# The gate columns as rows of the low-rank blocks, and the small products of the recurrences' chains in unbroken groups

## Chip, cores and metric

The kernel runs on one core of one Trainium2 chip. The metric is the device time of one launch in microseconds (us), as the median of the runs shown. The engines are TensorE (PE; its weight loads are listed apart as PEld), VectorE (DVE), ScalarE (ACT), GpSimd (POOL) and SyncE (SP), which issues most of the transfers.

## The reference, cut to what matters

Two blocks follow one another on a sequence of 512 tokens of width 2048. The first has a convolution branch and a differential attention and is not touched. The second joins a gated delta rule (GDN, 8 heads of 128) and an RWKV-7 recurrence (16 heads of 64), each in both directions, and each first over a context of 256 tokens and then, with the state that it left, over the 512 latent tokens:

```python
u = h @ w_in[layer]              # 512 tokens: GDN q, k, v, z (4 x 1024), 32 gate columns,
uc = hc @ w_in[layer]            # then RWKV r, k, v (3 x 1024), 4 x 96 low-rank columns, z
...
gates = u[..., 4 * D_GDN:].astype(jnp.float32).reshape(b, n, 2, 2, GDN_HEADS)
g = -jnp.exp(a_log) * jax.nn.softplus(gates[:, :, 0] + dt_bias)
beta = jax.nn.sigmoid(gates[:, :, 1])
...
def step(state, inp):            # gated delta rule, one chunk
    u_i, wk_i, attn_i, q_i, k_i, gl_i = inp
    v_new = u_i - wk_i @ state
    o_i = q_i @ state + attn_i @ v_new
    state = state * jnp.exp(gl_i)[..., None, None] + jnp.einsum('bhcd,bhce->bhde', k_i, v_new)
...
wd = xs[..., lo:lo + 2 * LORA_W].reshape(b, n, 2, LORA_W)     # RWKV: low-rank columns
ad = xs[..., lo + 2 * LORA_W:].reshape(b, n, 2, LORA_A)
w_log = -jax.nn.softplus(-(w0 + jnp.einsum('bndr,drc->bndc', jnp.tanh(wd), w_up))) - 0.5
a = jax.nn.sigmoid(a0 + jnp.einsum('bndr,drc->bndc', ad, a_up))
...
def step(state, inp):            # RWKV, one token; xs are mixed with their grid neighbours
    r_t, w_t, k_t, v_t, kk_t, b_t = inp
    sa = -jnp.einsum('bhvk,bhk->bhv', state, kk_t)
    state = (state * w_t[:, :, None, :] + sa[..., None] * b_t[:, :, None, :]
             + v_t[..., None] * k_t[:, :, None, :])
    return state, jnp.einsum('bhvk,bhk->bhv', state, r_t)
```

## The kernel before

**Dense products.** Every product with the weights `w_in` goes by `products` (L122 to L138) in blocks of 128 columns: SyncE loads half a block of weights (`wraw`), ScalarE rounds it (`whi`, L104) and VectorE takes the rest (`wlo`, L105; in the context stage every second one is GpSimd's, `K.on_pool = 2`). For each of the 16 tiles of 128 input rows, three products at L136 follow: whi by the high part of the activation, whi by its low part, wlo by the high part. A block is therefore 48 products of 128x512 (latent, activation `big`) or 128x256 (context, activation `hc`). `w2_cols` (L1756) makes 69 blocks of the second block's columns: one for the 32 gate columns (`B_GATE`, the other 96 columns empty), eight each for q, k, v, z of GDN and r, k, v of RWKV, four for the low-rank columns (`B_LO`, 96 columns and 32 empty ones each), eight for z of RWKV.

**The order.** A list scheduler puts each engine's instructions in order: of those whose inputs would be ready it takes the one with the lowest priority number, and that number grows along the program text. Dense products have `ahead = FIRST` for all but the first of a burst (6 or 12 products), so a burst stays together; small products of the chains have no such tie and are placed one by one between bursts. Each engine then runs its list strictly in that order.

**Gates.** `gdn_gates` (L420 to L517) takes a gate block from PSUM: VectorE adds the bias (gg_x, L425), works out softplus and logarithms by polynomials (L170 to L178, L427 to L444), makes a running sum over 64 tokens (L452 to L462) and writes three inputs gg_R (L467; L486 to L488 with ScalarE) of the transposes on TensorE (L497 to L499). Everything of the GDN chains waits on them.

**Low-rank blocks.** `rwkv_lora` (L793 to L799) mixes each block with its neighbours (ScalarE L771, VectorE L789) and puts the result aside. In the context stage the gate block comes first (L1697 to L1700), then K and V of GDN (`ctx_dense_gdn`), then the GDN chains, and behind them the low-rank blocks at the head of `ctx_dense_rwkv` (L1284). In the latent stage the gate block and the first low-rank block are multiplied while the activation is still being modulated (`K.pre`, L1450: PSUM banks px0 and pc); then follow gates, three low-rank blocks, and q, k, v, z head by head (`mixers_gdn`, L1485).

**GDN chains** (`gdn_core`, L700 to L758). A step takes 128 tokens in each direction: products with the state (L722), R on VectorE, products with the inverse (L728), vn on VectorE, products for the new state (L737), the state update on VectorE, and in the latent stream the output in a bank `po`: with the state (L751) and with vn (L752).

**RWKV chains** (`step` in `rwkv_pair`, L983 to L1058). One step takes 64 tokens of two heads (u) in both directions (d): four first products with the state H into bank `pc` (L1007), in the latent stream four output products into `po` (L1013), a copy X (ScalarE, L1016), four products with the inverse (L1032), H scaled by VectorE (L1034) and ScalarE (L1035), four products for the next state (L1039), four updates on VectorE that write the next H (L1047), and four more output products (L1052). There are 64 such steps in the latent stream and 32 in the context. Beside them the scheduler has the inversions of the next unit (L375, L381, 32x32), transposes (L931), 64x128 products (L964) and dense blocks to place. On the page each of the 64x64 products of these lines shows as two records.

## Time and profile before

| | |
|---|---|
| time, median of 3 runs | 3996.94 us (3995.03 to 4008.11) |
| profiled execution, its own time | 4009.06 us |
| span of that execution | 4007.3 us |
| busy: TensorE / VectorE / ScalarE / GpSimd | 3749.4 / 2758.9 / 1364.2 / 497.6 us |
| dense products of the first and second block together (L136), records with activation big | 5344 with whi, 2800 with wlo |
| mean granted clock of TensorE | 0.958 of full speed |

The profile lists one execution; all its times are microseconds from the span's start. A timeline row gives the start, how long from the first record's start to the last one's end, engine, line, tiles and the number of records; in brackets, where there is one, the idle time of that engine before it and what ended it. Matmul records overlap their successors, so what a product costs in the queue is the distance from its start to the next one's start. In the context stage the program runs from about 440 to 1580 us of the span, the latent front from 2200 to 2320, the latent chains from there on, RWKV's mostly from 3000 to 3890.

### The profile page before, as it was taken

Reading aid. Unit: us, or ns where it says so; the run is one execution under the profiler, and the core shown is the slowest. Engines: PE = TensorE matmul, PEld = TensorE weight load, DVE = VectorE, ACT = ScalarE, POOL = GpSimd, SP = SyncE. Lnnn points to the kernel's source line nnn. Section 1 sums busy time; section 2 is a strip of 40 time slices with the busy share of each in tenths; the row PEclk is TensorE's granted clock in tenths of the full one; section 3 lists DMA queues with packets and bytes.
Section 4 is the critical chain, followed back from the end, with each engine's and each line's share of the span. In section 5 each row is a group of like instructions: output and inputs, shape, how many; then the busy total and the mean of one; then the engine's idle time right before and its main releaser. Section 6 shows DMA issues by size and latency. Waiting matters only on the chain. (4 is left out here: it accounts for less than half of the span.)

```text
span 4007.3 us, 81999 instructions
## 1 busy us (share of the span) xinstructions
PE 3749.4 (94%) x33162; PEld 2890.2 (72%) x33162; DVE 2758.9 (69%) x7151; ACT 1364.2 (34%) x2707; POOL 497.6 (12%) x592
## 2 busy tenths in 40 slices
PE   8899779998999999999998799999999999999997
PEld 4577678876767677777886578777877777677776
DVE  3366897798777777643533977676667886777866
ACT  2322334322334434332322332232323443444433
POOL 0100230013100100000311201100001111110102
PEclk9899999999999999999999999999999998999999
DMA  8765445423324333524623232222223211122236
GB/s 318 259 231 212 155 135 168 146 100 112 120 79 142 108 110 110 168 85 163 210 95 125 98 103 71 68 71 68 83 80 108 68 65 56 67 72 89 98 124 203
DMA packets 206780, 495.05 MB, mean 124 GB/s; under 512 B 40129, under 2 KB 71361, under 8 KB 202305
## 3 DMA queue, kind: packets, MB, share of 16 engines
q1 hardware_dynamic: 206400, 489.81, 36.0%
q8 instruction: 260, 4.26, 0.4%
q14 instruction: 120, 0.97, 0.1%
HBM read 436.64 MB, written 53.09 MB: 122 GB/s over the span
## 5 line engine op out<-in xcount | busy, mean ns | idle before, releaser
L136 PE MATMUL pd<-big,whi 128*128 128x512 f32 x5344 | 1784.5, 412 | 9.3 <-ACT big L331 8.0
L136 PEld LDWEIGHTS pd<-big,whi 128*128 128x128 f32 x5344 | 980.5, 193 | 256.6 <-issue 20.4
L136 PE MATMUL pd<-big,wlo 128*128 128x512 f32 x2800 | 1120.1, 400 | 6.6 <-DVE wlo L105 6.2
L104 ACT CAST whi<-wraw 128x1024 fp32r<-128x1024 f32 (+2 forms) x500 | 506.7, 1014 | 1156.9 <-PE pd L136 1079.8
L105 DVE TENSOR_TENSOR wlo<-wraw,whi 128x1024 fp32r<-128x1024 f32 (+2 forms) x483 | 580.8, 1202 | 321.7 <-ACT whi L104 309.7
L136 PEld LDWEIGHTS pd<-big,wlo 128*128 128x128 f32 x2800 | 538.2, 192 | 130.6 <-DVE wlo L105 10.0
L136 PE MATMUL pd<-hc,whi 128*128 128x256 f32 x1184 | 229.5, 293 | 19.5 <-ACT gc_up L541 6.5
L136 PEld LDWEIGHTS pd<-hc,whi 128*128 128x128 f32 x1184 | 189.1, 195 | 24.1 <-ACT gc_up L541 7.2
L136 PE MATMUL pd<-hc,wlo 128*128 128x256 f32 x592 | 172.7, 292 | 25.8 <-DVE wlo L105 21.5
L136 PE MATMUL pd<-ext,whi 128*128 128x512 f32 x512 | 184.2, 400 | 3.9 <-DVE ext L105 3.8
L1133 DVE SCALAR_TENSOR_TENSOR cv_y<-cv_up,vec,cv_y 128x512 f32<-128x512 f32 x240 | 180.6, 752 | 4.4
L136 PE MATMUL pd<-fa,whi 128*128 128x512 f32 x448 | 149.9, 415 | 0.4 <-DVE wo L1520 0.2
L136 PEld LDWEIGHTS pd<-hc,wlo 128*128 128x128 f32 x592 | 115.3, 195 | 31.5 <-DVE wlo L105 25.1
L1029 ACT ACTIVATE rg_zw<-rg_H,rg_wc 64x64 f32<-64x64 f32 x320 | 104.6, 343 | 48.8 <-DVE rg_H L1047 43.4
L136 PEld LDWEIGHTS pd<-ext,whi 128*128 128x128 f32 x512 | 97.0, 190 | 27.8 <-DVE ext L105 4.8
L1047 DVE SCALAR_TENSOR_TENSOR rg_H<-pc,rg_wc,rg_zw 64x64 f32<-64x64 f32 x320 | 90.4, 283 | 35.7 <-PE pc L1039 27.1
L221 DVE SCALAR_TENSOR_TENSOR ada_ev<-wraw,cs_ada,ada_ev 128x512 f32<-128x512 f32 x120 | 90.7, 756 | 31.1 <-DMA wraw<-in_wada_dram 29.6
L546 DVE SCALAR_TENSOR_TENSOR gc_y<-gc_up,vec,gc_y 128x512 f32<-128x512 f32 (+1 forms) x160 | 106.8, 668 | 2.5
L916 POOL TENSOR_TENSOR rg_bk<-rg_th,rg_L 64x512 f32<-64x512 f32 x48 | 67.9, 1414 | 311.3 <-ACT rg_L L895 170.8
L136 PEld LDWEIGHTS pd<-fa,whi 128*128 128x128 f32 x448 | 80.3, 190 | 20.1 <-issue 1.4
L964 PE MATMUL px<-rg_C,rg_bk 64*128 64x128 f32 x512 | 90.5, 305 | 0.2 <-DVE rg_C L967 0.2
L1424 POOL TENSOR_TENSOR sgl<-sgl 128x512 f32<-128x512 f32 x16 | 33.9, 2118 | 448.1 <-ACT whi L104 441.2
(583 smaller groups left out, 5679.1 us busy)
## 6 DMA issues: line engine op xcount, KB each, us to landing
wraw<-in_w_dram SPq DMA_DIRECT2D x372, 512.0 KB, 3.6
wraw<-in_wada_dram SPq DMA_DIRECT2D x128, 512.0 KB, 4.6
wraw<-in_wada_dram SPq DMA_DIRECT2D x32, 1024.0 KB, 4.9
wraw<-in_wo_dram SPq DMA_DIRECT2D x32, 512.0 KB, 3.4
sgl<-sgd SPq DMA_DIRECT2D x48, 256.0 KB, 3.4
wraw<-in_wout_dram SPq DMA_DIRECT2D x20, 512.0 KB, 4.0
wraw<-in_w_dram SPq DMA_DIRECT2D x32, 256.0 KB, 3.6
sgd<-msg SPq DMA_DIRECT2D x32, 256.0 KB, 3.3
```

The source lines that it names most:

```text
L104: K.nc.scalar.copy(hi, src)
L105: (eng or K.nc.vector).tensor_tensor(lo, src, hi.bitcast(F32), op=ALU.subtract)
L136: nc.tensor.matmul(ps[:, :T], lhsT=a[:, k], rhs=b, start=(n == 0), stop=(n == 3 * (k1 - k0) - 1))
L221: nc.vector.scalar_tensor_tensor(ev, raw[:, k], cs[:, kk, 0:1], ev, op0=ALU.mult, op1=ALU.add)
L546: nc.vector.scalar_tensor_tensor(y, up[:, t:t + T], w[:, t:t + 1], y, op0=ALU.mult, op1=ALU.add)
L916: nc.gpsimd.tensor_tensor(bk[uq, :, u], th[uq], F[uq], op=mul)
L964: nc.tensor.matmul(pg[:, m], lhsT=bk[q, 4 * r + m].rearrange("p x c -> p (x c)"), rhs=C[q, 4 * r + m, u], start=True, stop=True, tile_posi ...
L1029: nc.scalar.activation(zw[hv[u], d], H[hv[u], ms[d], u], AF.Copy, scale=wn[hv[u], 4 * d + mn])
L1047: nc.vector.scalar_tensor_tensor(Hn[hv[u], 4 * d + mn, u], pc3[hv[u], 2, d], wn[hv[u], 4 * d + mn], zw[hv[u], d], op0=mul, op1=ALU.add)
L1133: nc.vector.scalar_tensor_tensor(y, up[:, t:t + 512], w[:, t:t + 1], y, op0=ALU.mult, op1=ALU.add)
L1424: nc.gpsimd.tensor_tensor(g, g, q, op=ALU.add)
```

## The change

**The gate columns move.** The block `B_GATE` is gone. Its 32 columns stand in the empty columns 96 to 103 of the four low-rank blocks, eight in each: decay gates of the two directions in the first two blocks, beta gates in the other two. `rwkv_lora` copies PSUM rows 96 to 127 of each block into a tile `gates` with ScalarE and mixes rows 0 to 95 as before. So the low-rank blocks come before the gates: in the context stage at the very front (`ctx_lora`), ahead of K and V; in the latent stage three of them (`PRE = 3`: banks px0, px1, pc) are multiplied during the modulation, and the fourth first thing afterwards. The second block has 68 weight blocks instead of 69.

**Small products are tied.** A class `Visit` issues the products of a group so that all but the first have `FIRST` (the scheduler takes them at once) and hang on the first by a dependence that orders without a semaphore. In RWKV the groups are L1007 with L1013, L1032 alone, L1039 with L1052; in GDN L722, L728, and L737 with L751 and L752. Within a group the order of d and u (j) is reversed, so that the product whose operand is written last comes first. `Visit.mm` is L123 of the changed kernel, and lines move: L136 is L157 there, L105 is L106, L381 is L402, L425 is L446, L497 to L499 are L518 to L520, L789 is L814.

```diff
+PRE = 3
-B_GATE, B_Q, B_K, B_V, B_Z, B_RR, B_RK, B_RV, B_LO, B_RZ = 0, 1, 9, 17, 25, 33, 41, 49, 57, 61
+B_Q, B_K, B_V, B_Z, B_RR, B_RK, B_RV, B_LO, B_RZ = 0, 8, 16, 24, 32, 40, 48, 56, 60
...
+class Visit:
+    def __init__(self, K):
+        self.K, self.first = K, None
+
+    def mm(self, *a, **kw):
+        tc = self.K.tc
+        ahead = FIRST if self.first else 0
+        tc.cur_priority -= ahead
+        i = self.K.nc.tensor.matmul(*a, **kw).ins
+        tc.cur_priority += ahead
+        if self.first:
+            tc.add_manual_dep(i, self.first.name, mybir.DependencyInfo(mybir.DependencyClass.NoSync,
+                                                                       mybir.DependencyReason.DATA), reason="visit")
+        else:
+            self.first = i
...
+        vis = Visit(K)
         if not (lat and fin):
             p = bank()
-            for d, j in chains:
-                nc.tensor.matmul(reg(p, d, j), lhsT=ktl[:, d, j, ts[d]], rhs=vn[d, j], start=True, stop=True)
+            for d, j in reversed(chains):
+                vis.mm(reg(p, d, j), lhsT=ktl[:, d, j, ts[d]], rhs=vn[d, j], start=True, stop=True)
+        if lat:
+            po = K.po.tile([128, 512], F32, name="po")
+            for d in (1, 0):
+                vis.mm(reg(po, d, 0), lhsT=vn[d, 0], rhs=at[:, d, ts[d]], start=True, stop=False)
+                vis.mm(reg(po, d, 0), lhsT=S[0][d], rhs=egt[:, d, 0, ts[d]], start=False, stop=True)
...
-def rwkv_lora(K, pool, blocks, T, s, put):
+def rwkv_lora(K, pool, blocks, T, s, put, gates):
     for j in range(4):
-        w = rwkv_mix(K, pool, blocks(B_LO + j), T, s, 3072 + 96 * j, 96, K.v["mulo"][:, j:j + 1], "rm", bufs=2)
+        ps = blocks(B_LO + j)
+        K.nc.scalar.copy(gates[32 * j:32 * j + 32], ps[96:128])
+        w = rwkv_mix(K, pool, ps, T, s, 3072 + 96 * j, 96, K.v["mulo"][:, j:j + 1], "rm", bufs=2)
...
-        for d in range(2):
-            for u in range(2):
-                nc.tensor.matmul(pc3[hv[u], 0, d], lhsT=C[:, ms[d], u, 0:64], rhs=H[:, ms[d], u], start=True, stop=True)
+        order = [(d, u) for d in (1, 0) for u in (1, 0)]
+        vis = Visit(K)
+        for d, u in order:
+            vis.mm(pc3[hv[u], 0, d], lhsT=C[:, ms[d], u, 0:64], rhs=H[:, ms[d], u], start=True, stop=True)
         if lat:
...
+            for d, u in order:
+                vis.mm(po[d][hv[u]], lhsT=H[:, ms[d], u], rhs=C[:, ms[d], u, 64:128], start=True, stop=False)
...
+        vis = Visit(K)
         if not fin:
...
+            for d, u in order:
+                vis.mm(pc3[hv[u], 2, d], lhsT=bt[:, ms[d], hv[u]], rhs=H[:, ms[d], u], start=True, stop=True)
+        if lat:
+            for d, u in order:
+                vis.mm(po[d][hv[u]], lhsT=H[hv[u], ms[d], u], rhs=ra[hv[u], ms[d]], start=False, stop=True,
+                       tile_position=(64 * u, 64 * u))
...
-            K.pre = {b: p.tile([128, 512], F32, name=n) for b, p, n in ((B_GATE, K.px, "px0"), (B_LO, K.pc, "pc"))}
+            K.pre = {B_LO + j: p.tile([128, 512], F32, name=n) for j, (p, n) in
+                     enumerate(((K.px, "px0"), (K.px, "px1"), (K.pc, "pc"), (K.pc, "pc"))[:PRE])}
...
-            gates = gdn_gates(K, pool, kp, blk(B_GATE), 512, "lat")
+            g = pool.tile([128, 512], F32, name="gates")
+            run(rwkv_lora(K, pool, blk, 512, "lat", lambda j, w: K.dma.dma_start(K.ld[:, j], w[:96]), g))
+            gates = gdn_gates(K, pool, kp, g, 512, "lat")
...
-                    K.gc = gdn_gates(K, pool, cl, blk(B_GATE), 256, "ctx")
+                    ctx_lora(K, blk, cl, pool)
                     ctx_dense_gdn(K, blk, pool)
...
-    g=-np.ones(128,int); 
-    for kind in range(2):
-        for d in range(2): g[64*kind+32*d:64*kind+32*d+8]=4096+16*kind+8*d+np.arange(8)
-    L.append(g)
...
-        x=-np.ones(128,int); x[:96]=R+3072+96*j+np.arange(96); L.append(x)
+        x=-np.ones(128,int); x[:96]=R+3072+96*j+np.arange(96); x[96:104]=4096+8*j+np.arange(8); L.append(x)
```

TensorE's list at one step of a latent RWKV chain (the bank pc_32152 is the step's, po_32157 and po_32160 are its output banks, rg_H its state, rg_C its factors, px1 a bank of an inversion), before:

```order
L381 MATMUL px1_32367<-iv_u32_32335,iv_y_32368 32x32 x19
L1007 MATMUL pc_32152<-rg_H_31419,rg_C_31406 64x64
L1013 MATMUL po_32157<-rg_C_31406,rg_H_31419 64x64
L1007 MATMUL pc_32152<-rg_H_31419,rg_C_31406 64x64
L1013 MATMUL po_32157<-rg_C_31406,rg_H_31419 64x64
L381 MATMUL px1_32367<-iv_u32_32335,iv_y_32368 32x32 x6
L1007 MATMUL pc_32152<-rg_H_31419,rg_C_31406 64x64
L1013 MATMUL po_32160<-rg_C_31406,rg_H_31419 64x64
L381 MATMUL px1_32367<-iv_u32_32335,iv_y_32368 32x32
L1007 MATMUL pc_32152<-rg_H_31419,rg_C_31406 64x64
L1013 MATMUL po_32160<-rg_C_31406,rg_H_31419 64x64
L381 MATMUL px1_32367<-iv_u32_32335,iv_y_32368 32x32 x6
```

The same step in TensorE's list now (its bank is pc_32052, its output banks po_32057 and po_32058; L123 is the tied product, L157 the dense one, L402 the inversion):

```order
L157 MATMUL pd_33054<-big_20583,wlo_33057 128x512
L123 MATMUL pc_32052<-rg_H_31319,rg_C_31306 64x64 x4
L123 MATMUL po_32058<-rg_C_31306,rg_H_31319 64x64 x2
L123 MATMUL po_32057<-rg_C_31306,rg_H_31319 64x64 x2
L402 MATMUL px1_32267<-iv_u32_32235,iv_y_32268 32x32 x17
L123 MATMUL pc_32052<-rg_X_32063,iv_u64_31561 64x64 x4
```

Eight products that stood in three places among the pieces of the inversion stand in one place now, behind a dense burst, and the inversion is no longer cut by them.

VectorE's list at the start of the latent gate arithmetic (big is the modulated activation, wlo a split of weights, gg_x the first step of the gates), before:

```order
L332 SCALAR_TENSOR_TENSOR big<-or_n,mod_ada_85,big 128x512
L105 TENSOR_TENSOR wlo<-wraw,whi 128x512
L105 TENSOR_TENSOR big<-or_n,big 128x512
L105 TENSOR_TENSOR wlo<-wraw,whi 128x512
L425 TENSOR_SCALAR gg_x<-px_20533,vec 64x512
L427 SCALAR_TENSOR_TENSOR gg_ax<-gg_x 64x512
```

Now (rm is a mixed low-rank block, gates the collected gate rows):

```order
L106 TENSOR_TENSOR big<-or_n,big 128x512
L794 TENSOR_SCALAR rm_omu<-vec 96x1 x2
L106 TENSOR_TENSOR wlo<-wraw,whi 128x512 x5
L814 SCALAR_TENSOR_TENSOR rm<-px_20477,vec,rm 96x448
L794 TENSOR_SCALAR rm_omu<-vec 96x1
L446 TENSOR_SCALAR gg_x<-gates,vec 64x512
L448 SCALAR_TENSOR_TENSOR gg_ax<-gg_x 64x512
L814 SCALAR_TENSOR_TENSOR rm<-px_20478,vec,rm 96x448
```

The gates' first step stands behind more splits of weights and behind the mix of the first low-rank block, and takes its input from a tile in place of a PSUM bank.

TensorE's list at the latent gate transposes (px are their banks, pd a dense block's), before, where the first two are followed by dense products again:

```order
L136 MATMUL pd<-big,wlo 128x512
L497 MATMUL px_20911<-cst,gg_R_20882 128x128
L497 MATMUL px_20916<-cst,gg_R_20882 128x128
L136 MATMUL pd<-big,whi 128x512 x2
L136 MATMUL pd<-big,wlo 128x512
```

And now, the first seven of them:

```order
L157 MATMUL pd<-big,wlo 128x512
L518 MATMUL px_21020<-cst,gg_R_20991 128x128
L518 MATMUL px_21025<-cst,gg_R_20991 128x128
L519 MATMUL px_21020<-cst,gg_R_20992 128x128
L519 MATMUL px_21025<-cst,gg_R_20992 128x128
L520 MATMUL px_21020<-cst,gg_R_20993 128x64
L520 MATMUL px_21025<-cst,gg_R_20993 128x64
L518 MATMUL px_21030<-cst,gg_R_20991 128x128
```

All twelve transposes stand together now, behind six blocks and more of the dense products, where ten of the twelve stood behind further dense products before.

## Rows read from the trace of the kernel before

**Rows 1.** Page, part 1: busy us of each engine, share of the span, instructions.
```profile
PE 3749.4 (94%) x33162; PEld 2890.2 (72%) x33162; DVE 2758.9 (69%) x7151; ACT 1364.2 (34%) x2707; POOL 497.6 (12%) x592
```
**Rows 2.** By stage: length, busy PE PEld DVE ACT POOL, granted clock, DMA share, GB/s.
```profile
440.00:640.00 200.00, 152.04 (x1103) 142.11 (x1104) 171.46 (x376) 74.99 (x124) 56.82 (x67) 0.91 0.42 138
...
2200.00:2320.00 120.00, 96.34 (x352) 66.95 (x351) 105.64 (x174) 46.78 (x67) 29.05 (x28) 0.90 0.34 109
...
3000.00:3700.00 700.00, 668.53 (x8784) 501.31 (x8782) 538.79 (x1607) 295.45 (x710) 91.36 (x80) 0.94 0.22 74
```
**Rows 3.** Timeline of TensorE, a latent RWKV step cut in three.
```profile
3302.64 0.34 PE L1007 MATMUL pc<-rg_H,rg_C 128*64 128x64 f32 x4
...
3303.03 0.31 PE L381 MATMUL px<-iv_u,iv_y 32*32 32x32 f32 x12
...
3303.82 0.33 PE L1007 MATMUL pc<-rg_H,rg_C 128*64 128x64 f32 x2
...
3304.20 0.31 PE L381 MATMUL px<-iv_u,iv_y 32*32 32x32 f32 x12
```
**Rows 4.** Timeline of TensorE, a latent RWKV step in one piece between dense products.
```profile
3329.06 0.40 PE L136 MATMUL pd<-big,wlo 128*128 128x512 f32 x1
3329.39 0.45 PE L1007 MATMUL pc<-rg_H,rg_C 128*64 128x64 f32 x8
...
3330.01 0.73 PE L136 MATMUL pd<-big,whi 128*128 128x512 f32 x2
```
**Rows 5.** Timeline of TensorE, a latent gated-delta step's third group.
```profile
2405.56 0.39 PE L136 MATMUL pd<-big,wlo 128*128 128x512 f32 x1
2405.79 0.61 PE L737 MATMUL pc<-gd_vn,gd_ktl 128*128 128x128 f32 x4
2406.23 0.39 PE L752 MATMUL po<-gd_at,gd_vn 128*128 128x128 f32 x2
2406.45 0.39 PE L751 MATMUL po<-gd_egt,S 128*128 128x128 f32 x2
```
**Rows 6.** By line and shape: busy us, mean ns of one, idle before, releaser.
```profile
L1047 DVE SCALAR_TENSOR_TENSOR rg_H<-pc,rg_wc,rg_zw 64x64 f32<-64x64 f32 x320 | 90.4, 283 | 35.7 <-PE pc L1039 27.1
```
**Rows 7.** Timeline of TensorE, two triples of a context low-rank block.
```profile
628.66 0.40 PE L136 MATMUL pd<-hc,whi 128*128 128x256 f32 x2
...
629.01 0.40 PE L136 MATMUL pd<-hc,whi 128*128 128x256 f32 x2
```
**Rows 8.** Timeline of ScalarE, context: last V block's copy, last low-rank block's mix.
```profile
604.38 0.37 ACT L541 COPY gc_up<-pd 128x256 f32<-128x256 f32 x1
...
634.31 0.47 ACT L771 ACTIVATE rm<-pd,rm_omu 96x256 f32<-96x256 f32 x1
```
**Rows 9.** Dense products with hc alone: length, busy TensorE, granted clock, DMA.
```profile
466.00:601.00 135.00, 97.07 (x717) 0.92 0.39 129
```
**Rows 10.** Timeline of TensorE, the context's first gate transposes.
```profile
501.07 0.69 PE L497 MATMUL px<-cst,gg_R 128*128 128x128 f32 x2 [5.95 <-DVE gg_R L467]
```
**Rows 11.** Timeline of VectorE, first step of the context's gate arithmetic.
```profile
461.50 0.48 DVE L425 TENSOR_SCALAR gg_x<-pd,vec 64x256 f32<-64x256 f32 x1 [0.60 <-PE pd L136]
```
**Rows 12.** Timeline of TensorE, latent front from the modulation's end to the transposes.
```profile
2262.52 0.61 PE L136 MATMUL pd<-big,whi 128*128 128x512 f32 x2
...
2264.66 0.62 PE L136 MATMUL pd<-big,whi 128*128 128x512 f32 x2
...
2296.66 0.62 PE L136 MATMUL pd<-big,whi 128*128 128x512 f32 x2
...
2302.15 0.69 PE L497 MATMUL px<-cst,gg_R 128*128 128x128 f32 x2 [4.66 <-DVE gg_R L467]
2302.49 1.20 PE L136 MATMUL pd<-big,whi 128*128 128x512 f32 x2
```
**Rows 13.** Timelines of VectorE and ScalarE, first and last step of the latent gates.
```profile
2260.06 0.74 DVE L425 TENSOR_SCALAR gg_x<-px,vec 64x512 f32<-64x512 f32 x1 [1.39 <-issue]
...
2305.51 0.63 ACT L488 ACTIVATE gg_R<-gg_tl 64x512 f32<-64x512 f32 x1 [0.58 <-DVE gg_tl L485]
```

More of the change, by code (lines that the diff above doesn't have):

```diff
@@ L726, in gdn_core @@
         p = bank()
-        for d, j in chains:
-            nc.tensor.matmul(reg(p, d, j), lhsT=uu[:, d, j, ts[d]], rhs=R[d, j], start=True, stop=True)
+        vis = Visit(K)
+        for d, j in reversed(chains):
+            vis.mm(reg(p, d, j), lhsT=uu[:, d, j, ts[d]], rhs=R[d, j], start=True, stop=True)
         vn = {}
@@ L733, in gdn_core @@
         new = {}
+        vis = Visit(K)
         if not (lat and fin):
             p = bank()
[L736 to L737 removed]
+            for d, j in reversed(chains):
+                vis.mm(reg(p, d, j), lhsT=ktl[:, d, j, ts[d]], rhs=vn[d, j], start=True, stop=True)
[4 more added lines that the diff above has]
+                vis.mm(reg(po, d, 0), lhsT=S[0][d], rhs=egt[:, d, 0, ts[d]], start=False, stop=True)
+        if not (lat and fin):
             for d, j in chains:
@@ L1050, in step @@
             for d in range(2):
-                for u in range(2):
-                    nc.tensor.matmul(po[d][hv[u], 0:64], lhsT=H[hv[u], ms[d], u], rhs=ra[hv[u], ms[d]], start=False,
-                                     stop=True, tile_position=(64 * u, 64 * u))
                 ot = osum[:, 64 * k:64 * k + 64] if d == 0 else osum[:, T - 64 * k - 64:T - 64 * k][:, ::-1]
                 if k < nch // 2:
-                    nc.scalar.copy(ot, po[d][:, 0:64])
+                    nc.scalar.copy(ot, po[d])
                 else:
-                    nc.vector.tensor_tensor(ot, po[d][:, 0:64], ot, op=ALU.add)
+                    nc.vector.tensor_tensor(ot, po[d], ot, op=ALU.add)
     def out():
```

54 lines of the change are left out of this document (22 added, 32 removed).

## Prediction

> **What bounds the kernel now.** The page comes first: TensorE is busy 94% of the span, the next engine, VectorE, 69% [rows 1]. A busy share is an average, so the second view is the table by stage [rows 2]; its columns to watch are TensorE, VectorE and the granted clock. In the long stage that holds the latent RWKV chains beside dense products (3000 to 3700 us) TensorE is busy 668.5 of 700 us, 96%, and VectorE 77%: what leaves TensorE's queue there shortens the kernel. Two short stages differ. From 440 to 640 us (the context's dense products) TensorE is busy 76% and VectorE 86%; from 2200 to 2320 us (norm, modulation, gate arithmetic of the latent stream) it is 80% and 88%. There a product taken from TensorE may only uncover VectorE. So the change is costed in three terms: the ties in the chains, the context's gate block, the latent gate block.
>
> **Term 1, the ties.** They add no instruction and take none away; they change the order of TensorE's queue. What a cut costs is read from a step that is cut in three [rows 3]: first products and first output products (L1007, L1013) stand as three visits between pieces of an inversion (L381). The first visit lasts 3303.03 - 3302.64 = 0.39 and the last 3304.20 - 3303.82 = 0.38 us; with the second, of as many records as the last, taken at 0.38 it is 1.15 together. The same sixteen records in one piece last 3330.01 - 3329.39 = 0.62 us [rows 4]. So two visits fewer save 0.53 us, 0.26 each. The way in costs as well: from the last dense product before the visit to its first record it is 3329.39 - 3329.06 = 0.33 us, where dense follows dense after a third of a triple, 0.68 / 3 = 0.23 us [rows 12]. With 0.10 to 0.14 for that a removed visit is worth up to 0.40 us. The number of visits I counted in both orders, a visit being an unbroken run of the products of one group: in the latent RWKV chains the first group stands in 124 visits before and 76 now, the second in 72 and 65, the third in 74 and 64; in the context's, the first in 63 and 33, the second in 35 and 32, the third in 32 both times. That is 98 fewer. At 0.26 it is 25.5 us, at 0.40 39 us. I take 26, the low end, since a removed visit whose neighbours then are dense and inversion pays the way in there all the same.
>
> The gated-delta chains are tied too (third group 64 visits to 32 in the latent stream). What a cut costs there has a row of its own: four products L737, then L752, L751, L752 and the next step's L722 and L751 go in between two dense pieces [rows 5], each pair of records taking 0.22 us (2406.45 - 2406.23), and the first starts 2405.79 - 2405.56 = 0.23 us after a dense product, as a dense product would. A cut of these products costs nothing that the rows show, so I put 0 us for this part; its upper bound is the 0.14 us above times 43 visits, 6 us.
>
> The Trainium skill, in TensorEngine Tiling (Array Packing), section Key Properties, says that a change of the array's tiling mode, not merely of the tile, drains the engine. By that rule the price hangs on changes of shape (128*128, 128*64, 64*64, 32*32), the gated-delta half (128*128, as the dense products) is worth nothing, and the third group keeps a change inside it however it is tied. Counted by shape, the orders hold 1741 changes before and 1566 now; 175 at about 0.15 us would be 26 us. The trace agrees in [rows 3] against [rows 5].
>
> Does a tie make TensorE wait? It runs its queue in order, so a group stands still until its last operand is there. The four updates that feed the next step take 283 ns each on VectorE [rows 6], and the tied group starts with the product whose operand is written last. Where it stands in the queue is counted from the orders: between a latent step's third group and the next step's first, 3.4 dense and 4.2 other products on average stand ahead of the first cut before, 4.2 and 6.5 ahead of the last cut; now 5.2 and 10.4 stand ahead of the whole group. So the group has gone to where its last cut stood or behind it; I put 0 for new waits and keep a rival for it. No engine's work is queued behind a new semaphore: the tie orders without a wait.
>
> **Term 2, the context's gate block.** The block of 48 products is gone, and the four low-rank blocks move ahead of the K and V blocks. A triple of dense products takes 0.355 us there (629.01 - 628.66), a block 16 times that, 5.7 us [rows 7]. Behind the V blocks the four low-rank blocks now stand from about 604.4 us (the last V block's copy gc_up) to 634.3 (the last mix) [rows 8]: 29.9 us, of which 4 x 5.7 = 22.8 is product time. That stretch goes. At the front TensorE has room: of the 135 us from 466 to 601 it spends 97.1 in dense products [rows 9], and its longest single wait there, 5.95 us at the gate transposes, is for VectorE [rows 10]. What the four blocks cost at the front is therefore VectorE's time. The gate arithmetic runs from 461.50 [rows 11] until the transposes at 501.07. By the placement of the gate columns its first step needs only the first two low-rank blocks (they carry the decay gates), so it starts later by less than one block, some 5 us; in its stretch VectorE's order now has five splits instead of four and three mixes more, 1.2 + 3 x 0.6 = 3 us. So the front ends 8 us later, and everything behind it too. Net: 8 - 22.8 = -14.8, at most 8 - 29.9 = -22; I take -15, because what follows has its own uneven start.
>
> **Term 3, the latent gate block.** A triple takes (2296.66 - 2264.66) / 47 = 0.68 us, a block 10.9 [rows 12]. Before, two blocks are multiplied during the modulation, then three low-rank blocks and six products of Q; then TensorE waits 4.66 us for gg_R [rows 12]. Now three low-rank blocks go during the modulation, then the fourth, the Q and the K block, and then the gate transposes, all twelve together. The third block adds 10.9 us to the modulation, of which some 3 us fill TensorE's gaps there: its end moves from 2262.52 to about 2270.4, and TensorE stands at the transposes at 2270.4 + 32.7 = 2303.1. VectorE's arithmetic from gg_x to gg_R took 2302.1 - 2260.06 = 42.0 us [rows 12, 13], with seven splits and three mixes among it; the new order has seven and three again. It starts some 7 us later, so gg_R is there at about 2309, and the last of the three inputs 4 us after it (2305.51 + 0.63 against 2302.15): TensorE waits until 2313, 10 us instead of 4.66. By then it has done 288 products that stay in the program, before it had 198 at 2302.15. 90 x 0.227 = 20.4 us of work for 10.9 us more time: a gain of 9.5 us; I take 9. Bounds: 2 us (arithmetic behind the fourth mix) and 14 (the wait as short as before). A long wait costs clock: after the 4.66 us the next pair of products lasts 1.20 us where a pair lasted 0.62 before [rows 12], which is the lower of the two levels; about 2 us of this is in the bounds.
>
> **What costs nothing.** Eight small copies of the gate rows on ScalarE, busy 34% [rows 1]; two blocks of weights (1 MB each) less to load, on a DMA share of 0.22 to 0.42 in these stages [rows 2].
>
> **Sum.** 26 + 15 + 9 = 50 us. The profiled execution took 4009.06 us, so its like would take 3959; the median before is 3996.94, and from it the forecast is 3997 - 50 = **3947 us**. Own range of this case: ends of the terms, 3930 to 3967.
>
> **Rivals.**
> - *The ties pay nothing.* If what costs is leaving the dense stream at all, then the ties don't do what they say: the stretches of small products between dense ones are 746 before and 756 now. Likewise if the time saved comes back as waits for the chains. Against it: the pieces in [rows 3] stand between small products and still cost. Left is 15 + 9 = 24: 3973 us.
> - *More than counted.* The way in is saved too (39 us), the whole 29.9 us goes in the context stage (22), and the latent block is fully gained (11): 72 us, 3925 us.
> - *The blocks are taken back and the ties half paid:* VectorE's arithmetic decides both front stages, the two terms give 24 - 24 = 0 and the ties 10: 3987 us.
> - *Slower: tied groups wait for their last operand.* Place: the first group of each of the 96 RWKV steps. If the group stands where its first piece stood, TensorE idles for three further updates, 3 x 0.283 = 0.85 us, 82 us over all; with 50 gained that is 3997 + 32 = 4029 us. It decides from 0.5 us of wait a step on. For it: VectorE, whose L1047 writes the state that L1007 reads, itself stands idle for TensorE's L1039 for 27.1 us in all [rows 6], so this loop is closed without slack in places. Against it: the counts above. The Trainium skill, TensorE: Matmul & The Clock Gate, Part 3, states that matmuls start and end strictly in program order; no row here shows otherwise.
>
> **How the numbers follow.** Forecast 0.55, ties pay nothing 0.19, more 0.12, taken back 0.07, slower 0.07. About 0.3% (12 us) is what a measurement of this kernel can tell from no change, that is 3985 to 4009. Faster beyond that are the first three, less a little for their edges: 0.85; the fourth makes most of 0.08 for no change; slower 0.07. A range of 8 in 10 must reach from the third case to the second and past its edge: 3920 to 3985; it leaves out the last two and the lower edge.
>
> **What would show it.** Right: first groups of eight and eight records in one piece lasting 0.62 us nearly everywhere; the last V copy of the context some 8 us later and the first mix of the RWKV blocks right behind it; a wait of about 10 us at the latent gate transposes; idle time before the tied products not above some 20 us in sum. Wrong: idle time before the tied products of 0.5 us a step or more, a lower granted clock from 3000 to 3700 us than 0.94, or a VectorE so late in the two fronts that the transposes wait 20 us and more.

## The result and the profile after

The changed kernel takes 3956.01 us (median of 6 runs, 3948.75 to 3974.94) where the kernel before took 4005.62 on the same occasion (6 runs, 3995.03 to 4012.71): a ratio of 0.989, 95% interval 0.9866 to 0.9914, or 44 us less by the ratio; the two medians lie 49.6 us apart. The forecast was 50 us less, 3947 us, in a range of 3920 to 3985. A second measurement of both kernels gave 0.9894 (0.9875 to 0.9914).

The page's first part and the table by stage of the changed kernel, to be laid beside [rows 1] and [rows 2] (length, busy PE, PEld, DVE, ACT, POOL, granted clock, DMA share, GB/s):

```profile
PE 3672.7 (93%) x33066; PEld 2837.3 (72%) x33066; DVE 2748.4 (70%) x7146; ACT 1359.4 (34%) x2713; POOL 505.4 (13%) x595
```
```profile
440.00:640.00 200.00, 160.38 (x1133) 150.09 (x1133) 167.25 (x327) 78.46 (x130) 64.35 (x68) 0.91 0.42 138
2200.00:2320.00 120.00, 107.15 (x454) 84.39 (x455) 95.59 (x188) 47.23 (x69) 14.90 (x25) 0.91 0.34 104
3000.00:3700.00 700.00, 650.16 (x9191) 487.19 (x9190) 567.18 (x1662) 298.41 (x734) 104.03 (x86) 0.95 0.23 75
```

TensorE is fuller in the two short stages (160 for 152 us, 107 for 96), as the moved blocks should make it, and emptier in the stage of the latent RWKV chains (650 for 668.5 us). There a fixed window holds other work in each kernel. The whole stage, from the last product of the gated-delta chains to the last of the RWKV chains, holds the same work; before and after:

```profile
3010.00:3888.00 878.00, 839.82 (x10975) 625.98 (x10973) 676.11 (x1965) 365.59 (x883) 112.55 (x96) 0.95 0.24 80
```
```profile
2965.00:3825.00 860.00, 804.00 (x10964) 603.35 (x10964) 673.17 (x1964) 360.39 (x880) 116.40 (x96) 0.95 0.24 80
```

TensorE is busy 36 us less, and the stage is 18 us shorter. What left the queue came back only in part as shorter time: the rest is waiting.

**Two measures that the rest needs.** The six runs of the changed kernel differ by 26 us, and the mean granted clock that each run lists goes with it. The profiled execution, and that of a second measurement of the same kernel (span and clock):

```profile
core 0: 3947.0 us, clock 0.962
```
```profile
core 0: 3969.0 us, clock 0.957
```

Time multiplied by clock was 3796 to 3803 us in all six runs, while the time went from 3949 to 3975. So for each kernel I give the *weighted time*, time by clock, as the mean of its runs less that of the runs of before beside them (standard errors 1 to 3 us). It compares the lists of instructions as if at one clock; a list that lowers its own clock gains nothing by that, so what is faster is decided by the plain ratio, which holds both. From each trace I also take *TensorE's work*, its busy stretches each multiplied by the clock granted there (the first 12 to 15 us of the span have no clock record; the 3 to 6 busy us in them are left out), and its *idle time*, the span less the busy time. Before: 3612.6 and 257.8 us. After: 3557.2 and 274.2, so 55.4 us less work and 16.4 us more waiting.

### The profile page after: what moved, and what is told of

It reads as the page before. It is cut to its first block, busy times and chain, and to the rows that moved or that the text cites. A ratio compares the mean times of both kernels' runs of the same rounds, so it can differ in the third digit from the quotient of the medians.

```text
span 3947.0 us, 81802 instructions
## 1 busy us (share of the span) xinstructions
PE 3672.7 (93%) x33066; PEld 2837.3 (72%) x33066; DVE 2748.4 (70%) x7146; ACT 1359.4 (34%) x2713; POOL 505.4 (13%) x595
## 5 line engine op out<-in xcount | busy, mean ns | idle before, releaser
L157 PE MATMUL pd<-big,whi 128*128 128x512 f32 x5280 | 1759.5, 411 | 8.0 <-ACT big L352 8.0
L157 PEld LDWEIGHTS pd<-big,whi 128*128 128x128 f32 x5280 | 964.4, 192 | 251.4 <-issue 20.8
L157 PE MATMUL pd<-big,wlo 128*128 128x512 f32 x2768 | 1104.2, 399 | 24.3 <-DVE wlo L106 23.6
L105 ACT CAST whi<-wraw 128x1024 fp32r<-128x1024 f32 (+2 forms) x498 | 502.9, 1010 | 1159.5 <-PE pd L157 1074.7
L106 DVE TENSOR_TENSOR wlo<-wraw,whi 128x1024 fp32r<-128x1024 f32 (+2 forms) x478 | 572.9, 1199 | 318.4 <-ACT whi L105 311.2
L157 PEld LDWEIGHTS pd<-big,wlo 128*128 128x128 f32 x2768 | 530.0, 191 | 147.1 <-DVE wlo L106 28.2
L157 PE MATMUL pd<-hc,whi 128*128 128x256 f32 x1152 | 227.0, 297 | 11.5 <-ACT hc L352 5.5
L157 PE MATMUL pd<-hc,wlo 128*128 128x256 f32 x576 | 171.7, 298 | 33.0 <-DVE wlo L106 23.9
L157 PEld LDWEIGHTS pd<-hc,whi 128*128 128x128 f32 x1152 | 188.3, 199 | 15.3 <-ACT hc L352 5.6
L157 PE MATMUL pd<-ext,whi 128*128 128x512 f32 x512 | 184.6, 401 | 3.8 <-DVE ext L106 3.8
L157 PE MATMUL pd<-fa,whi 128*128 128x512 f32 x448 | 149.9, 414 | 0.9 <-ACT fa L105 0.8
L157 PEld LDWEIGHTS pd<-hc,wlo 128*128 128x128 f32 x576 | 114.8, 199 | 40.0 <-DVE wlo L106 28.0
L1055 ACT ACTIVATE rg_zw<-rg_H,rg_wc 64x64 f32<-64x64 f32 x320 | 102.8, 342 | 43.4 <-DVE rg_H L1077 39.2
L157 PEld LDWEIGHTS pd<-ext,whi 128*128 128x128 f32 x512 | 97.3, 190 | 27.9 <-DVE ext L106 4.7
L157 PEld LDWEIGHTS pd<-fa,whi 128*128 128x128 f32 x448 | 80.7, 190 | 21.8 <-ACT fa L105 1.9
L157 PE MATMUL pd<-fa,wlo 128*128 128x512 f32 x224 | 89.1, 398 | 0.7 <-DVE wlo L106 0.7
L405 DVE COPY_PREDICATED iv_u<-cpi,px 128x256 f32<-128x256 int32 (+2 forms) x112 | 35.2, 340 | 73.2 <-PE px L402 62.8
```

Source lines behind the costliest of these rows:

```text
L105: K.nc.scalar.copy(hi, src)
L106: (eng or K.nc.vector).tensor_tensor(lo, src, hi.bitcast(F32), op=ALU.subtract)
L157: nc.tensor.matmul(ps[:, :T], lhsT=a[:, k], rhs=b, start=(n == 0), stop=(n == 3 * (k1 - k0) - 1))
L405: nc.vector.copy_predicated(u32[:, m0:m0 + w], K.cp[d, lev].unsqueeze(1).to_broadcast([128, w, 32]), zp[:, m0:m0 + w])
L1055: nc.scalar.activation(zw[hv[u], d], H[hv[u], ms[d], u], AF.Copy, scale=wn[hv[u], 4 * d + mn])
```

## The experiments

All twelve in one table; visits are those of the RWKV products in TensorE's list (400 before), changes are changes of the array's shape between successive matmul records of the four shapes 128\*128, 128\*64, 64\*64, 32\*32 in the trace (1283 before). The two columns on TensorE are differences from before.

| kernel | ratio, 95% interval | mean clock (before's) | weighted time | TensorE work | idle | visits | changes |
|---|---|---|---|---|---|---|---|
| changed, again | 0.9894 (0.9875–0.9914) | 0.9590 (0.9587) | -39.2 | -57.4 | +19.2 | 302 | 1174 |
| ties_only | 0.9944 (0.9922–0.9966) | 0.9622 (0.9598) | -15.2 | -36.0 | +19.7 | 302 | 1166 |
| gates_only | 0.9980 (0.9962–0.9999) | 0.9598 (0.9598) | -9.3 | -13.9 | +5.5 | 396 | 1278 |
| ties_rwkv | 0.9986 (0.9965–1.0007) | 0.9565 (0.9598) | -22.2 | -33.3 | +17.2 | 302 | 1166 |
| ties_gdn | 0.9976 (0.9950–1.0001) | 0.9633 (0.9598) | +5.4 | +1.4 | +3.7 | 401 | 1285 |
| split_ahead | 0.9927 (0.9903–0.9951) | 0.9562 (0.9587) | -38.2 | -56.4 | +11.3 | 302 | 1176 |
| ties_forward | 1.0051 (1.0035–1.0068) | 0.9537 (0.9587) | 0.0 | -15.2 | +11.9 | 410 | 1261 |
| ties_rwkv_gates | 0.9915 (0.9898–0.9932) | 0.9582 (0.9587) | -36.7 | -53.1 | +13.5 | 302 | 1178 |
| ctx_gates | 0.9904 (0.9879–0.9929) | 0.9617 (0.9597) | -28.5 | -44.5 | +13.0 | 302 | 1174 |
| front_pool | 0.9899 (0.9873–0.9924) | 0.9605 (0.9597) | -35.5 | -58.9 | +23.3 | 302 | 1174 |
| burst12 | 0.9993 (0.9978–1.0009) | 0.9500 (0.9597) | -40.5 | -69.5 | +38.6 | 296 | 1125 |
| reversed_untied | 0.9874 (0.9851–0.9897) | 0.9582 (0.9584) | -47.9 | -63.2 | +14.8 | 300 | 1165 |

**The two halves of the change, and the two halves of the ties.** Each of the four takes hunks of the diff as they stand and leaves the others out: `ties_only` has `Visit` and its uses in `gdn_core` and `step`, `ties_rwkv` and `ties_gdn` one of these, `gates_only` all the rest.

> The ties alone, the gate block left where it was. Theory (a removed visit of the RWKV products is worth 0.26 us, the gated-delta ties nothing): 302 visits instead of 400 in TensorE's list, 26 us faster than before. Rival (the profiled gain came from elsewhere, ties pay little, since a visit less inside a stretch of small products only moves the way in): 5 to 15 us faster. Rival (tied groups wait for their last operand): slower, with idle time before the tied products of over 30 us in sum.

> The gate columns moved, no ties. Theory: 24 us faster than before, 15 of it in the context (its last dense product some 15 us earlier) and 9 at the latent gates (more dense products done by the transposes). Rival (VectorE takes it back): within 10 us of before.

> The ties of the RWKV chains alone. Theory: the whole gain of the ties is theirs, 26 us faster than before, since the gated-delta products have the shape of the dense ones. Rival by count of stretches (740 here against 746 before): nothing, within 6 us of before.

> The ties of the gated-delta chains alone. Theory: 0, at most 6 us faster. Rival (a cut costs there too): 0.2 to 0.3 us for each of 43 visits fewer, 10 us faster. Rival (the groups of four to eight 128-wide products hold up the dense products for their last operand): slower by 5 us and more.

The ties make the kernel 22 us faster (0.9944), near the 26 expected; but as 36 us less work and 20 us more waiting, not as 26 and none. Nearly all of the work is the RWKV chains' (-33.3); the gated-delta ties take 43 visits out of the list and change TensorE's work by 1.4 us. So here a cut costs nothing that can be seen where the small product has the dense products' shape, and 98 removed visits of the RWKV products are worth 33.3 / 98 = 0.34 us of TensorE's work each, in the upper part of the forecast's 0.26 to 0.40. In plain time neither half alone is clear of no change, and they look equal, 0.9986 and 0.9976: the mean clock is 0.9565 with the RWKV ties and 0.9633 with the others, against 0.9598 before. The same stretch of the two kernels by stage, the RWKV ties first:

```profile
3000.00:3700.00 700.00, 654.82 (x8841) 492.56 (x8841) 550.11 (x1627) 300.43 (x724) 100.71 (x84) 0.93 0.23 76
```
```profile
3000.00:3700.00 700.00, 663.74 (x8892) 496.72 (x8892) 557.65 (x1649) 303.48 (x725) 99.18 (x86) 0.97 0.24 78
```

With its RWKV chains untied the second is busier (664 against 655 us), is granted 0.97 in place of 0.93, and gets through slightly more records in the same 700 us. The two profiles of the changed kernel alone differ there by half as much (0.95 and 0.93). Nothing that I changed in the gated-delta ties touches this stretch but the order in which lists reach it; why the clock differs stays open.

The gate columns alone gave 8 us of the 24 expected (0.9980; weighted 9.3). TensorE's work falls by 13.9 us, a little less than the two removed blocks (48 products of 0.227 us and of 0.118 us: 10.9 + 5.7 = 16.6), so a removed block saves about its own products.

The parts' weighted times add up to -24.5, the whole has -39.2. The 15 us between are real by the standard errors, and the traces place them in the context: from the start to the last dense product before the latent norm, work and idle together fall by 9.6 us with the gates, by 7.2 with the ties, and by 29.4 with both (28.2 in the second profile), 7 to 9 us of the surplus being idle time that neither part removes alone, as before the context's L1039 (8.3 us before; 6.9, 6.2 and, with both, 2.8). In the latent stages the parts add up within 3 us. The same holds in every kernel here that has both the reversed order of the RWKV products and the context's gate columns moved (25 to 31 us); `ties_forward` below, with the old order, has 12.7. What in the joint order closes these gaps I didn't find.

**The changed kernel again**, as a control for the runs beside it:

> The changed kernel once more, on the chip of the runs beside it. Theory (the parts add up to what the first six runs showed): 0.989 of the time before, 44 us faster, and 41 us less of time weighted with the granted clock. Rival (parts measured apart gave 24 and 8 us, so the whole is 32): 0.992.

0.9894, weighted -39.2: the theory, not the sum of the parts.

**Does the tie tie?** The products of a group in their old order, all else as changed:

```diff
-        order = [(d, u) for d in (1, 0) for u in (1, 0)]
+        order = [(d, u) for d in (0, 1) for u in (0, 1)]
...
-            for d, j in reversed(chains):
+            for d, j in chains:
```

> The changed kernel with the tied groups in their old order, so that the first product of a group is the one whose operand is ready first. Theory (a group is placed when its first product could start, and then stands for its later operands): idle time before the tied RWKV products rises by up to three updates of 0.283 us a step, and it is 10 to 60 us slower than the changed kernel. Rival (the group stands so far behind its operands in the list that the order within it doesn't matter): within 6 us.

It is slower than the kernel before (its weighted time is the same, its clock lower: 0.9537 against 0.9587), but not in the expected way: TensorE's idle time is 5 to 7 us lower than in the two profiles of the changed kernel, and before the RWKV products it is 9.3 us instead of 17.0. Its work is 40 to 42 us higher, and the list has 410 visits. A step of its first group on TensorE's timeline (L992 is a 64x128 product of the next unit):

```profile
3344.29 0.33 PE L123 MATMUL pc<-rg_H,rg_C 128*64 128x64 f32 x2
3344.55 0.49 PE L992 MATMUL px<-rg_C,rg_bk 64*128 64x128 f32 x2
3344.96 0.33 PE L123 MATMUL pc<-rg_H,rg_C 128*64 128x64 f32 x2
3345.22 0.48 PE L992 MATMUL px<-rg_C,rg_bk 64*128 64x128 f32 x2
3345.64 0.34 PE L123 MATMUL pc<-rg_H,rg_C 128*64 128x64 f32 x4
3345.90 0.48 PE L992 MATMUL px<-rg_C,rg_bk 64*128 64x128 f32 x2
3346.32 0.45 PE L123 MATMUL po<-rg_C,rg_H 128*64 128x64 f32 x8
```

The group (the products into pc and po) is in four pieces in spite of its tie. Priority only decides among products that could start; while the second waits for its state, the scheduler fills in something else. The last experiment is the counterpart: the reversed order with `ahead = 0` and without the dependence.

```diff
-        ahead = FIRST if self.first else 0
+        ahead = 0
...
-        if self.first:
-            tc.add_manual_dep(i, self.first.name, mybir.DependencyInfo(mybir.DependencyClass.NoSync,
-                                                                       mybir.DependencyReason.DATA), reason="visit")
-        else:
-            self.first = i
```

> The changed kernel with the groups in their reversed order, but with no tie: no priority and no dependence on the first product. Theory (the order from last-ready to first-ready is what leaves a group unbroken, since by the time its first product can be placed all others can too; the run with ties in the old order had 410 RWKV visits): 300 visits and 1689 changes of shape in TensorE's list against 302 and 1708, so TensorE time within 6 us of the changed kernel's and the time 0.987 to 0.992 of before. Rival (the tie does the work on the chip): 0.998, as with the gate columns alone.

300 visits, 0.9874, weighted -47.9: neither the priority nor the dependence is needed, and what the ties are credited with comes from the order in which the products are issued. That order differs from the kernel before in two ways: the groups are reversed, and the output products L1052, L751 and L752 are issued ahead of the updates instead of behind them. `ties_forward` has the second without the first, and 410 visits; the first without the second was not run. This kernel is the fastest of all twelve by weighted time, 9 us ahead of the changed kernel; in plain time the intervals overlap (0.9851 to 0.9897 against 0.9875 to 0.9914), so that it beats the changed kernel is likely and not settled.

**Where the waiting comes from.** The by-form rows of TensorE before and after (busy us, mean ns, idle before it and who ended that), for the first RWKV group and for the dense products with wlo:

```profile
L1007 PE MATMUL pc<-rg_H,rg_C 128*64 128x64 f32 x768 | 67.6, 242 | 5.5 <-DVE rg_H L1047 5.4
L136 PE MATMUL pd<-big,wlo 128*128 128x512 f32 x2800 | 1120.1, 400 | 6.6 <-DVE wlo L105 6.2
```
```profile
L123 PE MATMUL pc<-rg_H,rg_C 128*64 128x64 f32 x768 | 43.6, 235 | 7.5 <-DVE rg_H L1077 7.3
L157 PE MATMUL pd<-big,wlo 128*128 128x512 f32 x2768 | 1104.2, 399 | 24.3 <-DVE wlo L106 23.6
```

The first group's products into pc keep TensorE busy for 43.6 us instead of 67.6; before, they alternated with those into po, so that both rows count the same time. All RWKV products of a step together keep it busy for 170.3 us instead of 209.9 and wait 17.0 us instead of 20.6: the forecast's slower rival has no place here.

By stage, TensorE's idle time changes by -14.3 us in the context (start to the last dense product before the latent norm), +1.6 up to the gate transposes, +11.1 up to the end of the gated-delta chains and +17.8 in the RWKV stage. With the RWKV ties alone that last stage already has +15.5. There I find no single cause. The largest new waits are four, 8.8 us in sum, where TensorE is to transpose the inverse root that scales the RWKV output of a pair of heads (ro_rs_y) and VectorE isn't done with it. Before and after:

```profile
L288 PE MATMUL po<-cst,ro_rs_y 128*8 128x128 f32 x8 | 2.2, 272 | 0.0
```
```profile
L309 PE MATMUL po<-cst,ro_rs_y 128*8 128x128 f32 x8 | 2.3, 286 | 8.8 <-DVE ro_rs_y L175 8.8
```

No run here goes at these waits.

In the gated-delta stage the new waits are a dense product's, for its split of weights. They are five, each 4.5 us, in five of the eight heads. One on TensorE's timeline, and what VectorE did meanwhile:

```profile
2489.27 0.73 PE L157 MATMUL pd<-big,whi 128*128 128x512 f32 x2
2494.51 0.80 PE L157 MATMUL pd<-big,wlo 128*128 128x512 f32 x1 [4.51 <-DVE wlo L106]
2495.11 1.05 PE L157 MATMUL pd<-big,whi 128*128 128x512 f32 x2
```
```profile
2487.63 0.69 DVE L672 TENSOR_TENSOR gd_dd<-gd_dd,TM_lat 128x512 f32<-128x512 f32 x1
...
2489.85 0.69 DVE L207 SCALAR_TENSOR_TENSOR gq<-gc_th,gc_y 128x512 f32<-128x512 f32 x1
2490.45 0.68 DVE L1132 SCALAR_TENSOR_TENSOR gz<-gz,po 128x512 f32<-128x512 f32 x1
...
2493.24 1.22 DVE L106 TENSOR_TENSOR wlo<-wraw,whi 128x1024 fp32r<-128x1024 f32 x1
```

VectorE is not idle, it works through the next head's preparation and reaches the split last. Its rows show why: where a head's gd_dd is scaled (L672), the last split stands 42 instructions back and the next 15 ahead, in five heads; before, there is such a gap (67 and 12) in two, without such a wait. The wait costs clock too: the pair of products behind it lasts 1.05 us, where it lasts 0.62 elsewhere [rows 12], the lower of the two levels. Two experiments go at this, one that puts the splits ahead of all other work on VectorE and ScalarE during that stage, one that leaves the gated-delta ties out (hunks of the diff again). The first one's edit:

```diff
+    tc.cur_priority -= K.split_ahead
     split(K, hi[:, :w], lo[:, :w], raw[:, :w], nc.gpsimd if K.on_pool and K.n_split % K.on_pool == 0 else nc.vector)
+    tc.cur_priority += K.split_ahead
...
+            K.split_ahead = FIRST
             for i in range(8):
```

> The changed kernel with the splits of the dense weights put ahead of all other work on ScalarE and VectorE during the latent gated-delta stage. Theory (the tied gated-delta groups moved VectorE's list, so that a split stands 40 rows later and TensorE waits 4.51 us for it, five times): these five waits go, 22 us less idle time and 15 to 25 us faster than the changed kernel. Rival (the waits are only moved to the chains' products, since VectorE is late there anyway): within 6 us of it.

> The changed kernel without the gated-delta ties. Theory (these ties save no TensorE time and bring five waits of 4.5 us): idle time of TensorE falls by about 20 us in the latent stage, and the time weighted with the granted clock by 10 to 20 us. Rival (they raise the granted clock, as in the run with them alone, 0.9633 against 0.9598): the clock falls to about 0.957 without them and the plain time is the same or longer.

Both remove these waits (0.7 and 2.3 us are left of 23.3 in the latent part) and neither is faster: idle time falls by 5 to 8 and 3 to 6 us only, since other products wait instead, the chains' above all (with the splits ahead gd_dd's inversion goes from 5.6 to 11.9 us, and the product with the state, L722 before, from 0.0 to 5.6). So the rival of the first, that the waits are only moved, is near the truth, though for the inversion's waits the profile names no releaser. In plain time both are behind the changed kernel (0.9927 and 0.9915 against 0.9894); weighted they are within 2.5 us of it.

**The latent gate block.** The context as changed, the latent gates in a block of their own again (a 69th block of weights):

```diff
-            K.pre = {B_LO + j: p.tile([128, 512], F32, name=n) for j, (p, n) in
-                     enumerate(((K.px, "px0"), (K.px, "px1"), (K.pc, "pc"), (K.pc, "pc"))[:PRE])}
+            K.pre = {b: p.tile([128, 512], F32, name=n) for b, p, n in ((B_GATE, K.px, "px0"), (B_LO, K.pc, "pc"))}
```

> The changed kernel, but with the latent gate block kept as a block of its own, multiplied during the modulation as before; the context's gates and all ties as changed. Theory of the prediction (the latent block is worth 9 us): 9 us slower than the changed kernel. Rival, from the two profiles (the block's 10.9 us of products are saved, but TensorE waits nearly as much longer at the transposes and behind): within 3 us of it, with 10 us more TensorE time and 8 to 10 us less idle time.

TensorE has 11 to 13 us more work than in the two profiles of the changed kernel and 3 to 6 us less idle time; weighted it is 11 us slower, where the prediction's term said 9, in plain time 4 us (0.9904 against 0.9894) with intervals of 8 us and more, since its clock was 0.9617. Inconclusive between 4 and 11; the rival's 3 us is too low by the weighted time.

Every second split from the low-rank blocks to the first K block on GpSimd (`K.on_pool = 2` ahead of `rwkv_lora`, 0 behind the first K block):

> The changed kernel with every second split of dense weights given to GpSimd from the latent low-rank blocks to the first K block. Theory (VectorE's arithmetic decides when TensorE goes on at the latent gate transposes, and the splits stand in it): four splits of 1.2 us leave VectorE, the wait there shortens from 10.4 to about 6 us, and the kernel is 4 to 8 us faster. Rival (GpSimd's own split takes longer and TensorE waits for that, as for the context's blocks): within 3 us or slower.

No gain, 0.9899: the theory missed. The waits at the transposes are 10.0 us in sum instead of 10.4, and a split takes GpSimd 2.39 to 3.33 us, where VectorE needs 1.2.

**Longer bursts** beside the latent RWKV chains (`K.burst = 12` for 6 ahead of `mixers_rwkv`):

> The changed kernel with dense bursts of 12 products instead of 6 beside the latent RWKV chains. Theory (what the ties save is the change of the array's shape, 0.22 us each by the eight profiles so far): 1658 changes of shape instead of 1708, 11 us less TensorE time. Beside it the chains wait longer for their turn; the list has 3253 products left behind the last dense block of the stage instead of 1981, so idle time rises, and if by more than 11 us the kernel is slower. Rival (visits are what costs, not shapes): 296 instead of 302 visits, 2 us less TensorE time.

(The changes of shape are counted there over all shapes of results in the list, hence 0.22 us each; in the table's count it is 0.37.) TensorE's work falls by another 12 to 14 us (11 expected) with 49 changes fewer and the visits all but unchanged, and all of it is lost: idle time rises by 19 to 22 us and the clock falls to 0.950. The stretches from about the end of the last products with big on (3493 us in this kernel, 3622 in the changed one), in two parts each:

```profile
3480.00:3850.00 370.00, 336.80 (x4377) 251.47 (x4375) 283.32 (x815) 143.56 (x355) 47.55 (x42) 0.88 0.29 94
3850.00:3998.00 148.00, 108.56 (x1267) 86.89 (x1266) 93.94 (x239) 48.96 (x121) 25.76 (x33) 0.79 0.34 115
```
```profile
3620.00:3820.00 200.00, 186.92 (x2485) 137.94 (x2477) 151.65 (x406) 79.67 (x192) 24.60 (x18) 0.95 0.31 101
3820.00:3947.00 127.00, 103.95 (x572) 86.08 (x571) 77.09 (x149) 41.23 (x77) 26.09 (x33) 0.92 0.61 204
```

The dense products ran out early and the chains are left with less to stand beside them: before the RWKV products TensorE waits 41.1 us in all instead of 17.0. The clock granted in these stretches is 0.88 and 0.79 instead of 0.95 and 0.92 (0.90 and 0.92 in the second profile of the changed kernel).

## Why the prediction was right, point by point

**The sum** was 50 us and the result is 44, in the range and by the likeliest case. That the number fits so well is in part luck. Measured apart, the ties give 22 us and the gate columns 8, 30 of the 50; what brings them to 44 is a gain in the context that appears only with both (15 us weighted), which no term has and which isn't explained. The starting point, a median of three runs, also lay 9 us below that of six. And the forecast's own range, 3930 to 3967, isn't what the bounds of its terms add up to: 26 to 39, 15 to 22 and 2 to 14 us are 43 to 75, or 3922 to 3954.

**Term 1, the ties: 26 us less, at no new wait.** 22 us in plain time by the run with the ties alone, but the two steps behind it are both off. The price of a removed visit is 0.34 us of TensorE's work, not 0.26; that would fit if the way in, which I left out, is mostly saved too. A step in one piece is as read in [rows 4], 3305.87 - 3305.26 = 0.61 us, and so are most: in 56 of the 64 latent steps the first group's sixteen records stand in one piece (28 before).

```profile
3304.93 0.40 PE L157 MATMUL pd<-big,wlo 128*128 128x512 f32 x1
3305.26 0.45 PE L123 MATMUL pc<-rg_H,rg_C 128*64 128x64 f32 x8
3305.54 0.40 PE L123 MATMUL po<-rg_C,rg_H 128*64 128x64 f32 x8
3305.87 0.73 PE L157 MATMUL pd<-big,whi 128*128 128x512 f32 x2
```

The step that failed is "I put 0 for new waits": with the ties alone 20 us came back as idle time, 16 of them in the latent RWKV stage, not before the tied groups, where I had looked, but before what follows a chain and before the inversions. The zero for the gated-delta ties held for work (1.4 us). What the Trainium skill states in TensorEngine Tiling (Array Packing), section Key Properties, that a change of tiling mode "(not just tile)" drains the engine, agrees with that zero (43 visits, 1.4 us) and with burst12 (49 changes fewer, 6 visits fewer, 12 to 14 us of work). Over the 14 profiles, with the removed blocks' 16.6 or 5.7 us added back, TensorE's work follows the count of changes at 0.37 us each (correlation 0.98, no profile more than 8 us off). By itself this fit doesn't tell changes from visits, since the kernels fall into two groups, with and without the reversed order, and the count of visits correlates as well (0.98, 0.42 us each); burst12, from which a change is worth 0.25 to 0.29 us, and the gated-delta ties do. The prediction's 0.15 us was too low: its count of changes was over all shapes, 175, and by that the work saved, 55.4 - 16.6 = 38.8 us, is 0.22 each.

Of the prediction's signs, idle time before all the tied products was to be at most some 20 us; it is 25.6, above that, but the same products had 32.2 before. A granted clock below 0.94 from 3000 to 3700 us was to show it wrong: the first profile has 0.95 there, the second 0.93, so this sign doesn't decide.

**Term 2, the context's gate block: 15 us.** The last product with hc ends 17.3 us earlier (752.6 and 735.3 us of the span; 15.1 with the gates alone), near what the term said. Before and after:

```profile
752.34 0.28 PE L136 MATMUL pd<-hc,wlo 128*128 128x256 f32 x1
```
```profile
735.06 0.28 PE L157 MATMUL pd<-hc,wlo 128*128 128x256 f32 x1
```

The rows behind it, to be laid beside [rows 8 to 11]:

```profile
464.74 1.87 DVE L446 TENSOR_SCALAR gg_x<-gc_y,vec 64x256 f32<-64x256 f32 x1 [3.15 <-ACT gc_y L823]
```
```profile
466.00:601.00 135.00, 104.54 (x750) 0.94 0.41 134
```
```profile
507.22 0.58 PE L157 MATMUL pd<-hc,wlo 128*128 128x256 f32 x1 [4.30 <-DVE wlo L106]
...
510.49 0.69 PE L518 MATMUL px<-cst,gg_R 128*128 128x128 f32 x2 [0.76 <-DVE gg_R L488]
```
```profile
618.11 0.36 ACT L562 COPY gc_up<-pd 128x256 f32<-128x256 f32 x1
```

The gates start 3.2 us later and the transposes 9.4; 104.5 us of dense products instead of 97.1 fit into the same 135 us, and the wait of 5.95 us for the gates is 0.76, though 4.30 us of it have gone to a split. But the last V copy comes 13.7 us later, not 8, and the first inversion of the gated-delta chains too (644.5 and 658.2 us). The first mix of the RWKV blocks follows 12.8 us behind the copy, where the first low-rank mix followed before. The step that failed is "everything behind it": between the first and the last product with hc stand 490 records of other products instead of 715, and that work comes behind them now. With the gates alone the whole context gained 9.6 us (work and idle time), not 15; only together with the ties did it gain more.

**Term 3, the latent gate block: 9 us.** The profile is as forecast:

```profile
2275.49 0.69 PE L518 MATMUL px<-cst,gg_R 128*128 128x128 f32 x2 [6.42 <-DVE gg_R L488]
2279.41 0.66 PE L519 MATMUL px<-cst,gg_R 128*128 128x128 f32 x2 [3.23 <-DVE gg_R L507]
```

With a third gap of 0.75 us the transposes wait 10.4 us; the forecast was 10 instead of 4.66. From the end of the last product of the norm's squares to the first transpose it is 92.4 us where it was 81.4, 11.0 us more, for 90 products of 0.227 us that are done by then: 9.4 us. How much of this arrives at the end is between 4 and 11 us by ctx_gates. With the gates alone it is 3.0 us (work and idle time) at the end of the gated-delta chains and nothing at the end of the kernel. VectorE's arithmetic took 41.8 us (2275.43 - 2233.61) for 42.0.

**The rivals.** "Ties pay nothing" falls with ties_only. "More than counted" may be right about the way in, by the 0.34 us. "Taken back" was half right in mechanism: TensorE waits for VectorE in both fronts and in the gated-delta stage, and the blocks alone gave 8 of 24 us; over the whole span 16 of 55 us came back as idle time. "Slower by last-operand waits" is wrong: idle time before the RWKV products fell, 20.6 to 17.0 us; the order that would have invited it (ties_forward) is slower for another reason, cuts and clock.

## What to carry to other kernels

Products of one step that get their operands one after another are kept together by issuing them from the last-ready to the first-ready; a priority didn't do it here, because a list scheduler fills the gap while an operand is missing. What a cut costs depends on whether the array's shape changes, here some 0.25 to 0.37 us a change, so count changes of shape, not pieces. And on an engine that is 94% busy expect part of the freed time back as waits, here, in ten of the twelve kernels, between a fifth and over a half of it (`split_ahead` 11.3 of 56.4 us, `burst12` 38.6 of 69.5): cost a removed block at its own products, and look for whose list moved. Parts that are measured apart needn't add up: here 24.5 us weighted against 39.2.

## What was not expected of the hardware

The scatter of a kernel's times goes with its clock: six runs between 3949 and 3975 us have the same product of time and granted clock within 0.1% to either side. And the clock differs between orders of the list by as much as the changes themselves are worth: 0.9500 to 0.9633 over kernels with the same arithmetic to 0.5%, which is 1.4% or 55 us of time. In burst12 it is low where TensorE often waits, in the last 518 us; but that the gated-delta ties alone raised it from 0.960 to 0.963 (10 and 25 runs) has no such reason in the rows, and isn't explained.
